# Chaining VectorE's weight halves, first subtractions and query gates, and projecting tokens one weight tile at a time, in a two-branch decoder layer

## The chip, the core and the metric

The kernel runs on one core of a Trainium2 chip. A core has a matrix engine (TensorE, "PE" in the profile, with its weight loads shown apart as "PEld"), a vector engine (VectorE, "DVE"), a scalar engine (ScalarE, "ACT"), GpSimd ("POOL") and the queue that issues most DMAs (SyncE, "SP"). Each engine runs its own instructions in order and waits for the others by semaphores. The metric is the device time of one execution in microseconds (us); the figure that counts is the median of several executions.

## What is computed

One decoder layer over 512 tokens of width 1024. After an RMS norm, one input projection feeds two branches and two merge gates; the branches are projected up, merged, projected out and added to the input, and a gated embedding is added last:

```
h  = rmsnorm(x)
(attention q, k, v, gate | recurrence f, q, value, gate | merge gates) = h @ W_in
A  = block_sparse_attention(qknorm(q), qknorm(k), v, bias) * silu(gate)   # 8 heads x 64
R  = rmsnorm(hgrn2(q, keys from f, value, decay from f)) * silu(gate)      # 4 heads x 128
x  = x + (sigmoid(ga) * (A @ Ua) + sigmoid(gb) * (R @ Ub)) @ W_o
x  = x + gate(x @ W_g) * (p @ W_p)
```

Everything is float32. In the recurrence, a head has a decay per token and channel; the kernel works with its cumulative logarithm, over four blocks of 128 tokens.

## The kernel before

**Products.** A float32 product is made as three reduced products. Every weight tile `wf` (512 KB, two buffers, loaded by SP) is split into an upper half `wh` (a copy on ScalarE, line 184) and a lower half `wl` (a subtraction on VectorE, line 185), three buffers each; inputs are split the same way (`xh`, `xl`). Then xh·wh, xl·wh and xh·wl are summed in a PSUM bank. `weight` hands out the tiles in one fixed sequence and prepares each two tiles ahead of its use, so that the halves of tile i wait until TensorE is done with tile i-3.

**Stages.** TensorE's order is the order in which the program is written. First come the token-by-feature projections `bi` (the recurrence's values) and `av` (the attention's values), then decay and query of recurrence head 0 (`bf0`, `bq0`), then `aq` and `ak` (the attention's queries and keys). `proj_tok` makes each of these four in four PSUM banks, one per block of 128 tokens, from four weight tiles; a tile gives 24 matmuls, two contraction chunks by three products by four token blocks. After that come the feature-by-token projections, one bank each (`mm3`, 24 matmuls per weight tile), in the order of a table: gates, then `bf` and `bq` of heads 1 to 3 in between. Last come the up projections, the output projection and the embedding.

**Work put between.** Recurrence and attention are generators. Every matmul of a projection advances a clock (`tick`, 0.227 us for a 128x512 matmul); a generator says with `yield` after how much of that clock it goes on, and its matmuls are then written at that place. For a recurrence head h, `hgrn_gates` (lines 410 to 433) makes the cumulative decay `hu` (scans, line 428), the keys `hk` and the gated query `hq` (line 431, which is also the last reader of the bank of `bq`). `hgrn_intra` makes, for blocks of 64, 32, 8 and 2 tokens, differences of `hu` (the first subtractions, lines 447, 448, 460, 481, 484), their exponentials on ScalarE, and products with key and query (lines 450, 453, 487, 490); then `hkd` (lines 510 to 512). Small matmuls fill two banks, `lpb` and `lpa`. From these a tile `s` is assembled with seven predicated copies on VectorE (line 496), and `sc` with copies on ScalarE (lines 543, 546) and GpSimd (line 556). `hgrn_out` transposes `hkd` (`hktp`, line 565; copied to `hkt`, line 568), makes the block states (`hds`, line 573; `st` on VectorE, lines 577 and 580), and then the output (`hop`, lines 586 and 588), which needs both `sc` and `st`. `hms` (lines 601, 602) sums squares for a norm.

An attention step makes scores `s` on TensorE (line 700), the exponentials and their scaling `p` (lines 707 to 711), transposes them (`pt`, line 718) and copies them (`ptS`, line 722).

**What orders the other engines.** TensorE's order is written by hand. In the `bi` stage ScalarE's, VectorE's and SP's are too. Elsewhere a scheduler orders ScalarE, VectorE, GpSimd and SP: it places, by a model of the times, the ready instruction with the highest priority, which is its place in the program; inside `high_priority(offset=AHEAD)` an instruction counts as written 150 places earlier. Weight halves, `hgrn_gates` and the attention's `p` stand in such blocks.

**PSUM.** Eight banks: four ("mm") go round the projections, so that projection i waits for the readers of projection i-4; two ("g") go round the recurrence, so that `hktp` takes the bank of `lpb`, `hds` that of `lpa`, and `hop` that of `hktp`; two ("a") the attention.

Of the kernel before, what the change touches and what calls it, by code (L numbers as in the profile page):

```python
# [11 lines left out]
F32 = mybir.dt.float32  # L12
R = mybir.dt.float32r
I32 = mybir.dt.int32
AF = mybir.ActivationFunctionType
OP = mybir.AluOpType
# [5 lines left out]
NT = S // 128  # L22
# [18 lines left out]
LD = 2  # L41
# [9 lines left out]
AHEAD = 150  # L51
# [6 lines left out]
def hybrid_layer_kernel(  # L58
# [121 lines left out]
        A.activation(lb[:, 5], lb[:, 4], AF.Ln)  # L180


    def split(hi, lo, src):
        A.activation(hi, src, AF.Copy)  # L184
        V.tensor_tensor(lo, src, hi.bitcast(F32), op=OP.subtract)  # L185
# [36 lines left out]
    def w_split(upto):  # L222
        while len(wtile) <= min(upto, len(wseq) - 1):
            i = len(wtile)
            w_load(i)
            ap, kn, cols = wseq[i]
            hi = unit("wh", f"wh{i}", R, (128, kn, cols))
            lo = unit("wl", f"wl{i}", R, (128, kn, cols))
            with tc.high_priority(offset=AHEAD):
                split(hi, lo, wraw[i])  # L230
            wtile.append((hi, lo))

    def weight(ap, ahead=LD):
# [134 lines left out]
    def proj_tok(g, name, xh, xl, between=None):  # L368
        banks = [bank("mm", f"{name}{t}") for t in range(NT)]
        for kp in range(4):  # L370
            if between:
                between(kp)
                w2 = [weight(w_tok[g, kp], 0)]
                order = [(0, kk, t) for kk in range(2) for t in range(NT)]
                if kp == 3:
                    order = [(0, kk, t) for t in range(NT) for kk in range(2)]
            elif kp % 2 == 0:
                w2 = [weight(w_tok[g, kp]), weight(w_tok[g, kp + 1])]
                order = [(k2, kk, t) for t in (0, 1) for k2 in range(2) for kk in range(2)]
                order += [(k2, kk, t) for t in (2, 3) for k2 in range(2) for kk in range(2)]  # L380
            else:
                continue
            for k2, kk, t in order:
                wh, wl = w2[k2]
                k = 2 * (kp + k2) + kk
                s_ = slice(t * 128, t * 128 + 128)
                for i, (a, b) in enumerate(((xh[k], wh), (xl[k], wh), (xh[k], wl))):
                    PE.matmul(banks[t], a[:, s_], b[:, kk, :], start=(k == 0 and i == 0),  # L388
                              stop=(k == KD - 1 and i == 2))
                tick(0.681)  # L390
        return banks
# [19 lines left out]
    def hgrn_gates(h, F, Q):  # L411
        a = unit("H", f"ha{h}")
        A.activation(a, F, AF.Abs)
        A.activation(a, a, AF.Exp, scale=-1.0)
        A.activation(a, a, AF.Ln, bias=onec[:, 0:1])
        um = unit("H", f"hu{h}")
        V.tensor_scalar(um, F, -1.0, 30.0, op0=OP.mult, op1=OP.min)
        A.activation(um, um, AF.Exp)
        A.activation(um, um, AF.Ln, bias=onec[:, 0:1], scale=lbv[:, h:h + 1])
        V.scalar_tensor_tensor(a, F, 0.0, a, op0=OP.min, op1=OP.subtract)  # L420
        kb = unit("H", f"hk{h}")
        V.tensor_tensor(kb, a, F, op=OP.subtract)
        A.activation(kb, kb, AF.Exp, bias=ln1mlb[:, h:h + 1])
        V.tensor_tensor(a, a, um, op=OP.add)
        cum = um
        for c in range(NT):
            s_ = slice(c * 128, c * 128 + 128)
            V.tensor_tensor_scan(cum[:, s_], onec.to_broadcast([128, 128]), a[:, s_], 0.0, OP.mult, OP.add)
        sigmoid(a, Q)
        qm = unit("QM", f"hq{h}", shape=(128, 16, 48))  # L430
        V.tensor_tensor(qm[:, :, 0:32], a.rearrange("p (g t) -> p g t", t=32), Q.rearrange("p (g t) -> p g t", t=32),
                        op=OP.mult)
        hg[h] = (kb, qm, cum)

    def hgrn_intra(h):
# [3 lines left out]
        def halves(b):  # L439

            x = unit("Q", f"hx{h}_{b}")
            n = S // (2 * b)

            def v(t, half):
                return t.rearrange("p (n two b) -> p n two b", two=2, b=b)[:, :, half, :]
            ref = v(cum, 0)[:, :, b - 1:b].to_broadcast([128, n, b])
            V.tensor_tensor(v(x, 0), ref, v(cum, 0), op=OP.subtract)
            V.tensor_tensor(v(x, 1), v(cum, 1), ref, op=OP.subtract)
            A.activation(x, x, AF.Exp)
            V.tensor_tensor(v(x, 0), v(kb, 0), v(x, 0), op=OP.mult)  # L450
            xq = x.rearrange("p (n two g t) -> p n two g t", two=2, t=32, g=b // 32)[:, :, 1]
            qq = q.rearrange("p (n two g) t -> p n two g t", two=2, g=b // 32)[:, :, 1]
            V.tensor_tensor(xq, qq, xq, op=OP.mult)
            return x

        def near():

            c2 = cum.rearrange("p (g n two) -> p g n two", n=16, two=2)
            o = qm[:, :, 32:48]
            V.tensor_tensor(o, c2[:, :, :, 1], c2[:, :, :, 0], op=OP.subtract)  # L460
            A.activation(o, o, AF.Exp)
            V.tensor_tensor(o, q.rearrange("p g (n two) -> p g n two", two=2)[:, :, :, 1], o, op=OP.mult)

        def fours(b):


            kx = unit("Q", f"hkx{h}_{b}")
            qx = unit("QX", f"hqx{h}_{b}", shape=(128, 16, 48))
            n, m = S // (4 * b), 8 // b
            parts = [(d, 4 - d, e * b) for d, e in ((1, 0), (2, 3), (3, 5))]  # L470
            k4 = kx.rearrange("p (n f t) -> p n f t", f=4, t=b)
            c4 = cum.rearrange("p (n f t) -> p n f t", f=4, t=b)
            b4 = kb.rearrange("p (n f t) -> p n f t", f=4, t=b)
            q4 = q.rearrange("p g (m f t) -> p g m (f t)", m=m, f=4)
            x4 = qx.rearrange("p g (m e) -> p (g m) e", m=m)
            y4 = qx.rearrange("p g (m e) -> p g m e", m=m)
            G.memset(k4[:, :, 3, :], 0.0)

            def end(w):
                return c4[:, :, 0:w, b - 1:b].to_broadcast([128, n, w, b])  # L480
            V.tensor_tensor(k4[:, :, 0:3], end(3), c4[:, :, 0:3], op=OP.subtract)
            for d, w, e in parts:
                o = x4[:, :, e:e + w * b].rearrange("p n (f t) -> p n f t", t=b)
                V.tensor_tensor(o, c4[:, :, d:4], end(w), op=OP.subtract)
            A.activation(k4[:, :, 0:3], k4[:, :, 0:3], AF.Exp)
            A.activation(qx, qx, AF.Exp)
            V.tensor_tensor(k4[:, :, 0:3], b4[:, :, 0:3], k4[:, :, 0:3], op=OP.mult)
            for d, w, e in parts:
                o = y4[:, :, :, e:e + w * b]
                V.tensor_tensor(o, q4[:, :, :, d * b:4 * b], o, op=OP.mult)  # L490
            return kx, qx
# [15 lines left out]
        kd = unit("KT", f"hkd{h}", shape=(128, 3 * 128))  # L507
        cv = cum.rearrange("p (c t) -> p c t", c=NT)
        k3 = kd.rearrange("p (c t) -> p c t", c=3)
        V.tensor_tensor(k3, cv[:, 0:3, 127:128].to_broadcast([128, 3, 128]), cv[:, 0:3, :], op=OP.subtract)  # L510
        A.activation(kd, kd, AF.Exp)
        V.tensor_tensor(kd, kd, kb[:, :3 * 128], op=OP.mult)
        yield 2.5
# [22 lines left out]
            PE.matmul(lnr[p_, c, :], kb[:, o:o + 32], qm[:, 4 * c + g, :], start=True, stop=True)  # L536
        cost(1.5)
        A.activation(cum, cum, AF.Exp)
        V.tensor_tensor(s32, lnr[:, :, 0:32], eye[:, None, :].to_broadcast([128, NT, 32]), op=OP.mult)
        scv = sc.rearrange("p (i two) t -> p i two t", two=2)  # L540
        for par in range(2):
            i = 64 * par
            A.activation(scv[0:64, :, par, 64:128], big[i:i + 64, 0:2, :], AF.Copy)
            for half in range(2):
                j = 64 * half
                A.activation(scv[j:j + 32, :, par, j + 32:j + 64], big[i + 32 * half:i + 32 * half + 32, 2:4, 0:32], AF.Copy)
        for i, b in ((4, 8), (1, 2)):
            for d, e in ((1, 0), (2, 3), (3, 5)):
                pred(i + d - 1, lambda t: t.rearrange("p c (m e) -> p c m e", m=8 // b)[:, :, :, d * b:4 * b],
                     l4[b].rearrange("p c (m e) -> p c m e", m=8 // b)[:, :, :, e * b:(e + 4 - d) * b])  # L550
        pred(0, lambda t: t.rearrange("p c (n two) -> p c n two", two=2)[:, :, :, 1], lnr[:, :, 32:48])
        q12 = q[:, 4:16]
        V.tensor_tensor(q12, q12, cum[:, 128:].rearrange("p (g t) -> p g t", t=32), op=OP.mult)
        for g in range(4):
            s_ = slice(32 * g, 32 * g + 32)
            G.tensor_copy(sc[s_, :, s_], s32[s_])
        hg[h] += (kd,)

    def hgrn_out(h, vb):
        kb, qm, cum, kd = hg[h][:4]  # L560
        nk = 3 * 128
        yield 3.5
        kt = bank("g", f"hktp{h}")
        for c in range(3):
            PE.transpose(kt[:, c * 128:c * 128 + 128], kd[:, c * 128:c * 128 + 128], ident)
# [449 lines left out]
```

## Time and profile before

| | |
|---|---|
| time, median of 3 executions (lowest, highest) | 473.75 us (473.58, 474.74) |
| the profiled execution's own time | 474.0 us |
| its span, first to last instruction | 471.9 us |
| TensorE's mean granted clock | 0.999 |
| busy: TensorE / VectorE / ScalarE / GpSimd | 464.6 / 310.8 / 273.9 / 14.2 us |

The profiled execution spends 2.1 us outside its span. In the views, `MATMUL aq<-wh,xh` is an instruction that reads `wh` and `xh` and writes `aq`; buffer and head numbers are left out, so `hq` is that of any head, and times tell which. In a timeline a row is the start, the duration, and the idle time ahead of it with what ended it. TensorE overlaps matmuls: a 128x512 row lasts 0.39 us, and the next one starts 0.23 us after it, so its lateness is read from starts.

### The profile page before, as it was taken

Reading aid. Unit: us, or ns where it says so; the run is one execution under the profiler, and the core shown is the slowest. Engines: PE = TensorE matmul, PEld = TensorE weight load, DVE = VectorE, ACT = ScalarE, POOL = GpSimd, SP = SyncE. Lnnn points to the kernel's source line nnn. Section 1 sums busy time; section 2 is a strip of 40 time slices with the busy share of each in tenths; the row PEclk is TensorE's granted clock in tenths of the full one; section 3 lists DMA queues with packets and bytes.
Section 4 is the critical chain, followed back from the end, with each engine's and each line's share of the span. In section 5 each row is a group of like instructions: output and inputs, shape, how many; then the busy total and the mean of one; then the engine's idle time right before and its main releaser. Section 6 shows DMA issues by size and latency. Waiting matters only on the chain.

```text
span 471.9 us, 7256 instructions
## 1 busy us (share of the span) xinstructions
PE 464.6 (98%) x2776; PEld 384.8 (82%) x2776; DVE 310.8 (66%) x615; ACT 273.9 (58%) x479; POOL 14.2 (3%) x34
## 2 busy tenths in 40 slices
PE   9999999999999999999999999999999999999996
PEld 7888877888888778888788888888878888888886
DVE  4769696668989799849995466434459854543332
ACT  5857683478598789748885676554344522243201
POOL 0005000000000010000000100000000000000000
PEclk9999999999999999999999999999999999999999
DMA  7642222221541423231422233112534544322211
GB/s 228 218 145 90 90 89 90 89 90 50 172 145 59 141 85 90 90 111 47 131 91 92 90 101 102 47 62 53 188 95 138 193 145 147 109 93 95 91 44 46
DMA packets 19027, 50.42 MB, mean 107 GB/s; under 512 B 2352, under 2 KB 2992, under 8 KB 18992
## 3 DMA queue, kind: packets, MB, share of 16 engines
q1 hardware_dynamic: 18848, 49.95, 33.1%
q8 instruction: 22, 0.36, 0.3%
q14 instruction: 13, 0.11, 0.1%
q10 hardware_dynamic: 144, 0.01, 0.0%
HBM read 45.75 MB, written 2.10 MB: 101 GB/s over the span
## 4 chain that ended last, share of the span: by engine, by line
PE 87%; DVE 6%; ACT 5%; issue 1%; POOL 0%; DVEq 0%; POOLq 0%
PE ga L246 9%; PE g L246 9%; PE h L246 9%; PE gb L246 7%; PE bi L388 5%; PE ua L246 5%; PE ak L388 5%; PE ub L246 5%; PE av L388 5%; PE bg L246 5%; PE bf L246 4%; PE ag L246 3%; PE aq L388 3%; PE pe L246 2%; PE o L733 2%; PE s L700 2%
## 5 line engine op out<-in xcount | busy, mean ns | idle before, releaser
L184 ACT ACTIVATE wh<-wf 128x1024 fp32r<-128x1024 f32 (+1 forms) x81 | 77.5, 957 | 106.0 <-PE h L246 19.1
L185 DVE TENSOR_TENSOR wl<-wf,wh 128x1024 fp32r<-128x1024 f32 (+1 forms) x81 | 89.8, 1111 | 48.4 <-ACT wh L184 47.9
L707 DVE CUSTOM_DVE_ANT_0 p<-s,bias 128x128 f32<-128x128 f32 (+3 forms) x32 | 15.0, 486 | 21.8 <-PE s L700 21.7
L709 ACT ACTIVATE p<-p,ps 128x128 f32<-128x128 f32 (+3 forms) x32 | 17.7, 554 | 19.5 <-DVE ps L707 19.5
L246 PE MATMUL g<-hh,wh 128*128 128x512 f32 (+1 forms) x72 | 26.3, 365 | 0.0
L246 PE MATMUL g<-hl,wh 128*128 128x512 f32 (+1 forms) x72 | 26.3, 365 | 0.0
L246 PE MATMUL g<-hh,wl 128*128 128x512 f32 (+1 forms) x72 | 26.3, 365 | 0.0
L246 PE MATMUL gb<-xh,wh 128*128 128x512 f32 x64 | 26.3, 411 | 0.0
L246 PE MATMUL ga<-xh,wh 128*128 128x512 f32 x64 | 25.6, 400 | 0.0
L246 PE MATMUL gb<-xh,wl 128*128 128x512 f32 x64 | 25.1, 393 | 0.0
L246 PE MATMUL ga<-xh,wl 128*128 128x512 f32 x64 | 25.0, 391 | 0.0
L246 PE MATMUL gb<-xl,wh 128*128 128x512 f32 x64 | 25.0, 391 | 0.0
L246 PE MATMUL ga<-xl,wh 128*128 128x512 f32 x64 | 25.0, 390 | 0.0
L246 PE MATMUL h<-mh,wh 128*128 128x512 f32 x64 | 24.9, 390 | 0.0
L246 PE MATMUL h<-ml,wh 128*128 128x512 f32 x64 | 24.9, 389 | 0.0
L246 PE MATMUL h<-mh,wl 128*128 128x512 f32 x64 | 24.9, 389 | 0.0
L722 ACT ACTIVATE ptS<-pt 128x384 f32<-128x384 f32 (+1 forms) x24 | 12.5, 521 | 10.0 <-PE pt L718 9.8
L903 DVE TENSOR_TENSOR hf<-h,xres 128x512 f32<-128x512 f32 x8 | 5.5, 691 | 18.1 <-PE h L246 18.1
L246 PEld LDWEIGHTS g<-hh,wh 128*128 128x128 f32 x72 | 13.6, 189 | 2.2
L246 PEld LDWEIGHTS g<-hh,wl 128*128 128x128 f32 x72 | 13.6, 189 | 2.2
L246 PEld LDWEIGHTS g<-hl,wh 128*128 128x128 f32 x72 | 13.6, 189 | 2.1
L945 DVE TENSOR_TENSOR sg<-sg,pe 128x512 f32<-128x512 f32 (+1 forms) x9 | 5.6, 625 | 14.4 <-ACT sg L944 12.1
(319 smaller groups left out, 1265.2 us busy)
## 6 DMA issues: line engine op xcount, KB each, us to landing
wf<-in_w_tr_dram SPq DMA_DIRECT2D x32, 512.0 KB, 3.4
wf<-in_w_tok_dram SPq DMA_DIRECT2D x15, 512.0 KB, 3.3
wf<-in_w_up_dram SPq DMA_DIRECT2D x16, 256.0 KB, 2.7
wf<-in_w_o_dram SPq DMA_DIRECT2D x8, 512.0 KB, 3.3
wf<-in_w_g_dram SPq DMA_DIRECT2D x8, 512.0 KB, 3.3
bias<-in_brow_dram SPq DMA_DIRECT2D x8, 256.0 KB, 3.4
xres<-in_xT_dram SPq DMA_DIRECT2D x8, 256.0 KB, 2.8
xr<-in_xT_dram SPq DMA_DIRECT2D x7, 256.0 KB, 5.5
```

The lines of the kernel that those rows point to most:

```text
L184: A.activation(hi, src, AF.Copy)
L185: V.tensor_tensor(lo, src, hi.bitcast(F32), op=OP.subtract)
L246: PE.matmul(ps, a[:, k, :], b[k], start=(n == 0), stop=(n == tot - 1))
L388: PE.matmul(banks[t], a[:, s_], b[:, kk, :], start=(k == 0 and i == 0), stop=(k == KD - 1 and i == 2))
L700: PE.matmul(sp[:, o:o + nk], qn[h][:, qs], k_[:, :nk], start=(i == 0), stop=(i == 1))
L707: V.tensor_tensor_reduce(p_, sp[:, o:o + nk], T[:, nk - 1::-1], -1.0, 3e38, OP.add, OP.min, st[:, 0:1])
L709: A.activation(p_, p_, AF.Exp, bias=st[:, 0:1], scale=-1.0, accum_out=st[:, 1:2])
L722: A.activation(pt, tp[:, :n * 128], AF.Copy)
L733: PE.matmul(o[64 * j:64 * j + 64, qs], va[kb][:, h0:h0 + 64], pts[2 * hp + j, i][:, o0 + kb * 128:o0 + kb * 128 + 128], start=(kb == 0), s ...
L903: V.tensor_tensor(t, ps, xres, op=OP.add)
L945: V.tensor_tensor(t[:, :w], t[:, :w], pe[:, s_], op=OP.mult)
```

## The change

Three things are changed; no operation is added or removed.

1. On VectorE, the lower halves of the weights, the gated query `hq`, the first subtractions and the subtraction of `hkd` are tied together in the order in which they are written: `pin` tells the scheduler that each comes after the one before. It adds no wait to the engine, it only fixes their mutual order.
2. `proj_tok` takes for `av`, `aq` and `ak` one weight tile at a time and goes over its four token blocks. Before, it took two tiles together: token blocks 0 and 1 with both, then 2 and 3 with both. `bi` stays as it is, and each projection still has 96 matmuls.
3. The assembling of `s` and `sc` at the end of `hgrn_intra` counts as written 150 places earlier, the GpSimd copies are written ahead of the product of line 553, and `hgrn_out` waits 5.0 instead of 3.5 us of the clock before `hktp`.

```diff
+    def pin(op):
+        if pinned[0] is not None:
+            tc.add_manual_dep(op.ins, pinned[0].name,
+                              mybir.DependencyInfo(mybir.DependencyClass.NoSync, mybir.DependencyReason.DATA))
+        pinned[0] = op.ins
...
             with tc.high_priority(offset=AHEAD):
-                split(hi, lo, wraw[i])
+                A.activation(hi, wraw[i], AF.Copy)
+                pin(V.tensor_tensor(lo, wraw[i], hi.bitcast(F32), op=OP.subtract))
...
-            elif kp % 2 == 0:
-                w2 = [weight(w_tok[g, kp]), weight(w_tok[g, kp + 1])]
-                order = [(k2, kk, t) for t in (0, 1) for k2 in range(2) for kk in range(2)]
-                order += [(k2, kk, t) for t in (2, 3) for k2 in range(2) for kk in range(2)]
...
+            wh, wl = weight(w_tok[g, kp], 0 if between else LD)
+            order = [(kk, t) for t in range(NT) for kk in range(2)]
...
-        V.tensor_tensor(qm[:, :, 0:32], a.rearrange("p (g t) -> p g t", t=32), Q.rearrange("p (g t) -> p g t", t=32),
-                        op=OP.mult)
+        pin(V.tensor_tensor(qm[:, :, 0:32], a.rearrange("p (g t) -> p g t", t=32),
+                            Q.rearrange("p (g t) -> p g t", t=32), op=OP.mult))
...
-            V.tensor_tensor(v(x, 0), ref, v(cum, 0), op=OP.subtract)
-            V.tensor_tensor(v(x, 1), v(cum, 1), ref, op=OP.subtract)
+            pin(V.tensor_tensor(v(x, 0), ref, v(cum, 0), op=OP.subtract))
+            pin(V.tensor_tensor(v(x, 1), v(cum, 1), ref, op=OP.subtract))
...
-        V.tensor_tensor(s32, lnr[:, :, 0:32], eye[:, None, :].to_broadcast([128, NT, 32]), op=OP.mult)
+        with tc.high_priority(offset=AHEAD):
+            V.tensor_tensor(s32, lnr[:, :, 0:32], eye[:, None, :].to_broadcast([128, NT, 32]), op=OP.mult)
...
-        yield 3.5
+        yield 5.0
         kt = bank("g", f"hktp{h}")
```

**VectorE while `aq` runs.** The two pieces are VectorE's instructions behind the scans of head 0. `wl12` and `wl13` are the lower halves of the third and fourth weight tile of `aq`; `hq0` at L431 (now L434) is the gated query. Before:

```order
L428 SCALAR_TENSOR_TENSOR hu0_600<-onec_85,ha0_596 128x128 x4
L510 TENSOR_TENSOR hkd0_870<-hu0_600 128x384
L185 TENSOR_TENSOR wl12_625<-wf12_622,wh12_624 128x1024
L447 TENSOR_TENSOR hx0_64_674<-hu0_600 128x4x64
...
L512 TENSOR_TENSOR hkd0_870<-hkd0_870,hk0_605 128x384
L431 TENSOR_TENSOR hq0_616<-ha0_596,bq0_571 128x16x32
...
L490 TENSOR_TENSOR hqx0_8_766<-hq0_616,hqx0_8_766 128x16x8
L462 TENSOR_TENSOR hq0_616<-hq0_616 128x16x16
L185 TENSOR_TENSOR wl13_631<-wf13_628,wh13_630 128x1024
L185 TENSOR_TENSOR wl14_692<-wf14_689,wh14_691 128x1024
```

Now:

```order
L431 SCALAR_TENSOR_TENSOR hu0_600<-onec_85,ha0_596 128x128 x4
L434 TENSOR_TENSOR hq0_616<-ha0_596,bq0_571 128x16x32
L240 TENSOR_TENSOR wl12_625<-wf12_622,wh12_624 128x1024
L240 TENSOR_TENSOR wl13_655<-wf13_652,wh13_654 128x1024
L450 TENSOR_TENSOR hx0_64_674<-hu0_600 128x4x64
L451 TENSOR_TENSOR hx0_64_674<-hu0_600 128x4x64
L453 TENSOR_TENSOR hx0_64_674<-hk0_605,hx0_64_674 128x4x64
L456 TENSOR_TENSOR hx0_64_674<-hq0_616,hx0_64_674 128x4x64
L240 TENSOR_TENSOR wl14_692<-wf14_689,wh14_691 128x1024
```

`hq0` stands right behind the scans instead of 17 rows later, `wl13` right behind `wl12` instead of 29 rows later, and the work of `hgrn_intra` comes after both.

**TensorE in head 1.** The transposition `hktp1` and what stands around it, at the change from `bq2` to `gb1`. Before:

```order
L700 MATMUL s12_1703<-kl1_1267,qs1_1004 128x384
L565 MATMUL hktp1_1714<-ident_87,hkd1_1575 128x128 x3
L246 MATMUL bq2_1588<-xh7_421,wh26_1467 128x512
L246 MATMUL bq2_1588<-xl7_422,wh26_1467 128x512
L246 MATMUL bq2_1588<-xh7_421,wl26_1468 128x512
L674 MATMUL ktp1_1723<-ident_87,kr0_1119 128x128
```

Now:

```order
L704 MATMUL s12_1703<-kl1_1267,qs1_998 128x384
L256 MATMUL bq2_1588<-xh7_415,wh26_1467 128x512
L256 MATMUL bq2_1588<-xl7_416,wh26_1467 128x512
L256 MATMUL bq2_1588<-xh7_415,wl26_1468 128x512
L256 MATMUL gb1_1745<-xh0_384,wh27_1524 128x512
L256 MATMUL gb1_1745<-xl0_385,wh27_1524 128x512
L256 MATMUL gb1_1745<-xh0_384,wl27_1525 128x512
L678 MATMUL ktp1_1749<-ident_87,kr0_1119 128x128
L678 MATMUL ktp1_1749<-ident_87,kr1_1124 128x128
L678 MATMUL ktp1_1749<-ident_87,kr2_1129 128x128
L678 MATMUL ktp1_1749<-ident_87,kr3_1134 128x128
L569 MATMUL hktp1_1766<-ident_87,hkd1_1575 128x128 x3
```

`hktp1` has moved behind six 128x512 matmuls and the four transpositions `ktp1`; `hds1` then follows twelve matmuls later, as before it followed after nine of `gb1` and the three of `bq2`.

**ScalarE in head 1.** The copies `hkt1` and `kh2`, the upper half `wh29` and the exponential of `p12`. Before:

```order
L722 ACTIVATE ptS03_1689<-pt03_1684 128x512
L568 ACTIVATE hkt1_1718<-hktp1_1714 128x384
L486 ACTIVATE hqx2_2_1975<-hqx2_2_1975 128x768
L184 ACTIVATE wh29_1764<-wf29_1762 128x1024
L251 ACTIVATE ha2_1740<-bq2_1588 128x512
L188 ACTIVATE kh2_1728<-ktp1_1723,sm_66 64x512
```

Now:

```order
L726 ACTIVATE ptS03_1689<-pt03_1684 128x512
L426 ACTIVATE hk2_1726<-hk2_1726,lb_95 128x512
L239 ACTIVATE wh29_1741<-wf29_1739 128x1024
L713 ACTIVATE p12_1706,ps12_1707<-p12_1706,ps12_1707 128x384
L261 ACTIVATE ha2_1717<-bq2_1588 128x512
L197 ACTIVATE kh2_1754<-ktp1_1749,sm_66 64x512
L572 ACTIVATE hkt1_1770<-hktp1_1766 128x384
```

`hkt1`, on which `hds1` waits, has moved from the front to behind `wh29`, the exponential, `ha2` and `kh2`.

More of the change, by code (lines that the diff above doesn't have):

```diff
@@ L180, in lower_bound @@
         A.activation(lb[:, 5], lb[:, 4], AF.Ln)
+    pinned = [None]
+    def pin(op):
[3 more added lines that the diff above has]
+        pinned[0] = op.ins
     def split(hi, lo, src):
@@ L372, in proj_tok @@
                 between(kp)
[L373 to L376, printed above, removed]
-            elif kp % 2 == 0:
-                w2 = [weight(w_tok[g, kp]), weight(w_tok[g, kp + 1])]
-                order = [(k2, kk, t) for t in (0, 1) for k2 in range(2) for kk in range(2)]
-                order += [(k2, kk, t) for t in (2, 3) for k2 in range(2) for kk in range(2)]
[L381 to L385, printed above, removed]
+            wh, wl = weight(w_tok[g, kp], 0 if between else LD)
+            order = [(kk, t) for t in range(NT) for kk in range(2)]
+            if between and kp < 3:
+                order = [(kk, t) for kk in range(2) for t in range(NT)]
+            for kk, t in order:
+                k = 2 * kp + kk
                 s_ = slice(t * 128, t * 128 + 128)
@@ L459, in near @@
             o = qm[:, :, 32:48]
-            V.tensor_tensor(o, c2[:, :, :, 1], c2[:, :, :, 0], op=OP.subtract)
+            pin(V.tensor_tensor(o, c2[:, :, :, 1], c2[:, :, :, 0], op=OP.subtract))
             A.activation(o, o, AF.Exp)
@@ L480, in end @@
                 return c4[:, :, 0:w, b - 1:b].to_broadcast([128, n, w, b])
-            V.tensor_tensor(k4[:, :, 0:3], end(3), c4[:, :, 0:3], op=OP.subtract)
+            pin(V.tensor_tensor(k4[:, :, 0:3], end(3), c4[:, :, 0:3], op=OP.subtract))
             for d, w, e in parts:
                 o = x4[:, :, e:e + w * b].rearrange("p n (f t) -> p n f t", t=b)
-                V.tensor_tensor(o, c4[:, :, d:4], end(w), op=OP.subtract)
+                pin(V.tensor_tensor(o, c4[:, :, d:4], end(w), op=OP.subtract))
             A.activation(k4[:, :, 0:3], k4[:, :, 0:3], AF.Exp)
@@ L509, in hgrn_intra @@
         k3 = kd.rearrange("p (c t) -> p c t", c=3)
-        V.tensor_tensor(k3, cv[:, 0:3, 127:128].to_broadcast([128, 3, 128]), cv[:, 0:3, :], op=OP.subtract)
+        pin(V.tensor_tensor(k3, cv[:, 0:3, 127:128].to_broadcast([128, 3, 128]), cv[:, 0:3, :], op=OP.subtract))
         A.activation(kd, kd, AF.Exp)
@@ L538, in hgrn_intra @@
         A.activation(cum, cum, AF.Exp)
-        V.tensor_tensor(s32, lnr[:, :, 0:32], eye[:, None, :].to_broadcast([128, NT, 32]), op=OP.mult)
[L540 to L551, printed above, removed]
+        with tc.high_priority(offset=AHEAD):
+            V.tensor_tensor(s32, lnr[:, :, 0:32], eye[:, None, :].to_broadcast([128, NT, 32]), op=OP.mult)
+            scv = sc.rearrange("p (i two) t -> p i two t", two=2)
+            for par in range(2):
+                i = 64 * par
+                A.activation(scv[0:64, :, par, 64:128], big[i:i + 64, 0:2, :], AF.Copy)
+                for half in range(2):
+                    j = 64 * half
+                    A.activation(scv[j:j + 32, :, par, j + 32:j + 64], big[i + 32 * half:i + 32 * half + 32, 2:4, 0:32], AF.Copy)
+            for i, b in ((4, 8), (1, 2)):
+                for d, e in ((1, 0), (2, 3), (3, 5)):
+                    pred(i + d - 1, lambda t: t.rearrange("p c (m e) -> p c m e", m=8 // b)[:, :, :, d * b:4 * b],
+                         l4[b].rearrange("p c (m e) -> p c m e", m=8 // b)[:, :, :, e * b:(e + 4 - d) * b])
+            pred(0, lambda t: t.rearrange("p c (n two) -> p c n two", two=2)[:, :, :, 1], lnr[:, :, 32:48])
+            for g in range(4):
+                s_ = slice(32 * g, 32 * g + 32)
+                G.tensor_copy(sc[s_, :, s_], s32[s_])
         q12 = q[:, 4:16]
         V.tensor_tensor(q12, q12, cum[:, 128:].rearrange("p (g t) -> p g t", t=32), op=OP.mult)
-        for g in range(4):
-            s_ = slice(32 * g, 32 * g + 32)
-            G.tensor_copy(sc[s_, :, s_], s32[s_])
         hg[h] += (kd,)
```

## The prediction

> **What bounds the kernel now.** I read the page first: busy times and the chain that ended last.
>
> ```profile
> PE 464.6 (98%) x2776; PEld 384.8 (82%) x2776; DVE 310.8 (66%) x615; ACT 273.9 (58%) x479; POOL 14.2 (3%) x34
> PEclk9999999999999999999999999999999999999999
> PE 87%; DVE 6%; ACT 5%; issue 1%; POOL 0%; DVEq 0%; POOLq 0%
> ```
>
> TensorE is busy 464.6 of 471.9 us at full granted clock in every slice. The change leaves its matmuls as they are, so it can only win back waits, of which there are at most 471.9 - 464.6 = 7.3 us, part of them at the start. The second view is TensorE's waits:
>
> ```profile
> PE aq L388 <- DVE wl L185: 0.9, 1, 0.9
> ...
> PE hop L586 <- POOL sc L556: 0.7, 1, 0.7
> PE hktp L565 <- DVE s L496: 0.5, 1, 0.5
> PE pt L718 <- DVE p L711: 0.4, 1, 0.4
> PE aq L388 <- DVE hq L431: 0.2, 1, 0.2
> ```
>
> Each is one event. The left-out one is the warm-up at the start, which the change doesn't touch. All five end on VectorE, the fourth GpSimd step standing itself behind VectorE's `s`. As matmuls overlap, idle time understates a delay; I take it from the starts in TensorE's timeline, an undisturbed 128x512 matmul starting 0.23 us after the one before (69.24 to 69.47):
>
> ```profile
> 61.53 0.39 PE L388 MATMUL aq<-wh,xh 128*128 128x512 f32 x1
> ...
> 69.24 0.39 PE L388 MATMUL aq<-wh,xl 128*128 128x512 f32 x1
> 69.47 0.39 PE L388 MATMUL aq<-wl,xh 128*128 128x512 f32 x1
> 70.01 0.50 PE L388 MATMUL aq<-wh,xh 128*128 128x512 f32 x1 [0.16 <-DVE hq L431]
> 70.35 0.39 PE L388 MATMUL aq<-wh,xl 128*128 128x512 f32 x1
> ...
> 74.46 0.39 PE L388 MATMUL aq<-wh,xl 128*128 128x512 f32 x1
> 75.78 0.50 PE L388 MATMUL aq<-wl,xh 128*128 128x512 f32 x1 [0.93 <-DVE wl L185]
> ...
> 84.98 0.39 PE L388 MATMUL ak<-wh,xh 128*128 128x512 f32 x1
> ```
>
> The first wait delays 70.01 - 69.47 - 0.23 = 0.31, and the matmul behind it comes 0.34 instead of 0.23 later, so 0.42. The second: 75.78 - 74.46 - 0.23 = 1.09, and with the same 0.11 behind it 1.20.
>
> **Part 1, `aq` (chain and single tiles).** Why these two were late, on VectorE and then on ScalarE:
>
> ```profile
> 69.28 0.68 DVE L431 TENSOR_TENSOR hq<-ha,bq 128x512 f32<-128x512 f32 x1
> ...
> 72.16 2.10 DVE L490 TENSOR_TENSOR hqx<-hq,hqx 128x384 f32<-128x384 f32 x6
> ...
> 74.51 2.35 DVE L185 TENSOR_TENSOR wl<-wf,wh 128x1024 fp32r<-128x1024 f32 x2
> ```
>
> ```profile
> 64.43 0.63 ACT L253 ACTIVATE ha<-ha 128x512 f32<-128x512 f32 x1
> ...
> 71.47 1.07 ACT L184 ACTIVATE wh<-wf 128x1024 fp32r<-128x1024 f32 x1 [1.21 <-PE aq L388]
> ```
>
> `aq3` takes the bank of `bq0`, whose last reader is `hq0`. `hq0` ran from 69.28 to 69.96, though its sigmoid was done at 64.43 + 0.63 = 65.06. Pinned right behind the scans it ends at 65.06 + 0.68 = 65.74 at the latest. But the single tile also brings `aq3` forward: not 36 but 18 matmuls into the stage, 61.53 + 18 x 0.227 = 65.6. So the wait is 0 to 0.2 plus 0.11 behind it; as `hkd0`'s exponential has left the middle of the sigmoid on ScalarE, I take 0. If something else delays the sigmoid by the length of a `wh`, it costs 1.1: the upper bound.
>
> `wl13` waits for `wh13`, which waits for TensorE to leave tile 10. In pairs it left that tile after 42 matmuls, at 71.4 (the row's releaser says so); alone it leaves it after 24, at 61.53 + 24 x 0.227 = 67.0. `wh13` then ends at 68.2 and `wl13`, no longer behind the products of `hqx0`, at about 69.5. Single tiles need it after 72 matmuls, at 77.9: 8 us to spare. Gain 1.20, and nothing in `ak` that should take its place: what moves behind `wl13`, `hgrn_intra` of head 0, has until `lpb0`, in the middle of `ak`, and I follow its products only to 88, some 4 us into it.
>
> `av` needs nothing either: `wl7` now falls between two steps of the norm and delays it by one half, 1.2, but the transposition of the norm stands 2.5 us behind its input and the last `xl` has 3 us.
>
> **Part 2, attention in head 1 (chain).** TensorE and, below it, VectorE:
>
> ```profile
> 155.08 0.39 PE L246 MATMUL bf<-xh,wl 128*128 128x512 f32 x1
> 155.83 0.52 PE L718 MATMUL pt<-ident,p 128*128 128x128 f32 x3 [0.37 <-DVE p L711]
> ```
>
> ```profile
> 155.27 0.42 DVE L711 TENSOR_SCALAR p<-p,ps 128x384 f32<-128x384 f32 x1
> ```
>
> Lateness 155.83 - 155.08 - 0.23 = 0.52. The scaling of `p02` stood behind `wl26`; a whole weight half costs
>
> ```profile
> L185 DVE TENSOR_TENSOR wl<-wf,wh 128x1024 fp32r<-128x1024 f32 x62 | 76.8, 1241 | 46.7 <-ACT wh L184 46.3
> ```
>
> 1.24 us, more than the lateness. In the new order it stands in front of `wl26` and of the products of the blocks of 8. Gain 0.52.
>
> **Part 3, `hktp1` (priority and yield).** TensorE, then VectorE:
>
> ```profile
> 167.86 0.34 PE L700 MATMUL s<-kl,qs 128*128 128x384 f32 x1
> 168.71 0.52 PE L565 MATMUL hktp<-ident,hkd 128*128 128x128 f32 x3 [0.51 <-DVE s L496]
> ```
>
> ```profile
> 166.38 0.69 DVE L424 TENSOR_TENSOR ha<-ha,hu 128x512 f32<-128x512 f32 x1 [0.30 <-ACT hu L419]
> ...
> 167.12 1.36 DVE L428 TENSOR_TENSOR_SCAN hu<-onec,ha 128x128 f32<-128x128 f32 x4
> 168.40 0.17 DVE L496 COPY_PREDICATED s<-mkf,lpb 128x32 f32<-128x32 int32 x1
> ```
>
> `hktp1` takes the bank of `lpb1` and waited for the third predicated copy, behind four scans; without the wait it would have started at 168.03, so 0.68 lost. It now comes six matmuls and four transpositions later: 168.03 + 6 x 0.23 + 0.44 = 169.8 (0.11 a transposition, from the three of `hktp1` that took 0.28 to the next start), against a copy that ends by 169.1 even behind all scans. Gain 0.68.
>
> What is late next is `hkt1`, on which `hds1` waits. `hds1` now comes at 169.8 + 0.28 + 12 x 0.23 = 172.8. ScalarE does ahead of it `wh29`, the exponential of `p12`, `ha2` and `kh2`:
>
> ```profile
> 169.27 0.49 ACT L568 ACTIVATE hkt<-hktp 128x384 f32<-128x384 f32 x1 [1.69 <-PE hktp L565]
> ...
> 170.57 1.04 ACT L184 ACTIVATE wh<-wf 128x1024 fp32r<-128x1024 f32 x1
> 171.53 0.57 ACT L251 ACTIVATE ha<-bq 128x512 f32<-128x512 f32 x1
> 172.00 0.67 ACT L188 ACTIVATE kh<-ktp,sm 64x512 fp32r<-64x512 f32 x1
> ...
> 173.61 0.61 ACT L709 ACTIVATE p<-p,ps 128x384 f32<-128x384 f32 x1
> ```
>
> With `hkt1` that is 1.04 + 0.61 + 0.2 (reading the sum) + 0.57 + 0.67 + 0.49 = 3.6 us. `wh29` can start when `bq2` is through (168.03 + 3 x 0.23 and about 0.2 to its end: 168.9), or up to 0.6 later if the exponential waits for VectorE: `hkt1` ends between 172.5 and 173.1. So `hds1` waits -0.3 to +0.3; if `wh29` starts no earlier than before (170.57), 174.2 and a wait of 1.3. Taken: 0.2.
>
> **Part 4, `hop2` (priority and yield).** TensorE, VectorE, GpSimd:
>
> ```profile
> 225.41 0.49 PE L718 MATMUL pt<-ident,p 128*128 128x128 f32 x3
> 226.57 0.71 PE L586 MATMUL hop<-sc,biv 128*128 128x128 f32 x4 [0.67 <-POOL sc L556]
> ```
>
> ```profile
> 224.83 0.29 DVE L496 COPY_PREDICATED s<-mkf,lpa 128x64 f32<-128x64 int32 x1
> ```
>
> ```profile
> 225.25 1.27 POOL L556 COPY sc<-s 32x128 f32<-32x128 f32 x4 [33.77 <-DVE s L496]
> ```
>
> Three transpositions take 0.24 to 0.28, so `hop2` was due at 225.65 and lost 0.92. In the new order the last predicated copy of `s2` no longer has a weight half ahead of it, and that alone (1.24) pays the 0.92; and `hop2` stands 13 matmuls, 2.9 us, later. The state `st2` is then the later of its two inputs: copied on VectorE about 4.2 us after `hds2` starts, and due 4.9 after it. Gain 0.92, with 0.7 to spare. For `hop1` the same sum leaves no more than 0 to 0.1, since `wl29` (1.24) stands ahead of `st1`. Heads 0 and 3 have over 2 us.
>
> **Sum.** 0.42 + 1.20 + 0.52 + 0.68 + 0.92 = 3.74 removed; 0.2 added at `hds1` and 0.0 to 0.1 at `hop1`: net 3.5. From the profiled execution's 474.0 that is 470.5; it lies 0.25 above the median, so on the median's footing 470.25. I write 470.3. The extreme where each part goes as well as it can, with a few of the 0.1 us gaps in `ak` going too, is 469.5.
>
> **Rivals.**
> *B, the recurrence's waits come back.* Only `aq` is cured (1.62), while `hds1`, `hop1` and `hop2` wait again, for `hkt` and `st` now, about as long as `pt02`, `hktp1` and `hop2` do today: 473.75 - 1.62 = 472.1. For it: the inputs now in question come from ScalarE and VectorE queues that hold a weight half right ahead of them, and slacks of 0 to 0.7 are less than one such half. Against: the scheduler's order leaves the five old delays with 1 us or more.
> *C, slower: a chained order that waits.* A pinned `wl` waits for its `wh`, and that for TensorE; all that stands behind it on VectorE waits along, the `p` and `st` that TensorE needs next too. A row above shows the mechanism: at 166.38 VectorE stood idle 0.30 for ScalarE, while predicated copies of finished banks stood behind. The price is a pair of halves, 1.04 + 1.24 = 2.3, for each place. Two such places in heads 1 to 3 eat the gain (4.6 - 3.7 = +0.9, 474.6), three make it slower: 6.9 - 3.7, 476.9. For it: VectorE has little room to catch up there,
>
> ```profile
> 136.59:196.00 59.41, 58.53 (x407) 48.49 (x406) 55.26 (x145) 49.52 (x98) 1.81 (x6) 1.00 0.30 95
> ```
>
> 55.26 busy of 59.41 us (third figure). Against: tile i needs only tile i-3 to be left, 5.4 us ahead of its own use, so that `wl` has 3 us even when it comes last. [...]
> *D, the change misses its places.* `aq3`, brought forward, waits on `hq0` for up to 1.1, and two of the other three gains are replaced: 1 us net, 472.7.
>
> **Numbers.** No change is what lies within 0.3% (1.42 us: 472.3 to 475.2), about what a measurement of this kernel can tell. The forecast has 0.60, B 0.20, D 0.11, C 0.09. Faster: the forecast, and of B and D together 0.13: 0.73. Slower: two thirds of C, and something unforeseen, 0.07. The same: 0.20. Eight in ten lie between 469.5 and 473.0, which takes in B and D and leaves out C; the forecast's own range is 469.5 to 471.5.
>
> **What would show it.** In TensorE's waits of the changed kernel the five rows above should be gone, and no row for `hds` or `hop` should exceed 0.3. `aq` should last 96 x 0.227 = 21.8 from its first start to that of `ak`, where it lasts 84.98 - 61.53 = 23.45 now; if it lasts 22.5, `hq0` is late (D). `wl13` should follow `wl12` at about 69.5. In head 1, `hkt1` should end within 0.3 of when `hds1` is due; if it ends at 174, ScalarE's order decides (B). A wait of `pt` or `s` on `p` or `ptS` of over 1 us in heads 1 to 3 with VectorE idle ahead of a `wl` would be C. What would make me wrong most easily is the hand-made time of `hkt1` and `st1`, whose slack is smaller than the error of such a reckoning.

## The result: 469.9 us, and the profile after

The changed kernel takes 469.90 us in the median of four executions (469.51 to 470.19), against 473.89 us before (473.58 to 474.74, four executions): a ratio of 0.9912, with a 95% interval of 0.9895 to 0.993. The forecast was 470.3. The profiled execution took 469.64 us, its span is 467.7 instead of 471.9. Of the page, the busy times and the chain that ended last:

```profile
PE 462.7 (99%) x2776; PEld 385.2 (82%) x2776; DVE 311.6 (67%) x615; ACT 274.6 (59%) x479; POOL 12.6 (3%) x34
...
PE 95%; DVE 2%; ACT 1%; DMA 1%; SPq 0%; issue 0%; DVEq 0%
```

All engines do the same instructions as before, in nearly the same busy time (GpSimd 12.6 for 14.2 us); VectorE and ScalarE have gone from 11% of the chain to 3%. TensorE's waits are now these two, the second of 0.2 us:

```profile
PE warm L147 <- PEq L1006: 0.8, 1, 0.8
PE hms L606 <- DVE htl L194: 0.2, 1, 0.2
```

All five rows on which the sum rested are gone, and a small one has come. TensorE's timeline of the changed kernel at the end of `bi`, at the start of `aq`, where `aq3` begins, at the start of `ak`, and at `hms0`:

```profile
27.54 0.39 PE L391 MATMUL av<-wh,gh 128*128 128x512 f32 x1
...
61.18 0.39 PE L391 MATMUL aq<-wh,xh 128*128 128x512 f32 x1
...
65.03 0.39 PE L391 MATMUL aq<-wl,xh 128*128 128x512 f32 x1
65.25 0.45 PE L391 MATMUL aq<-wh,xh 128*128 128x512 f32 x1
65.54 0.40 PE L391 MATMUL aq<-wh,xl 128*128 128x512 f32 x1
...
83.04 0.39 PE L391 MATMUL ak<-wh,xh 128*128 128x512 f32 x1
...
113.76 0.39 PE L605 MATMUL hms<-hth,ones 128*128 128x512 f32 x1
114.40 0.50 PE L606 MATMUL hms<-htl,ones 128*128 128x512 f32 x1 [0.25 <-DVE htl L194]
```

`aq` lasts 83.04 - 61.18 = 21.86 instead of 23.45: 1.59 of the 4.24 that TensorE's last matmul comes earlier. `hms0` gives back 0.27. The three waits of heads 1 and 2 (2.12 as forecast) and the small gaps around them make 2.47. And 0.36 lies in `bi`, which the change doesn't touch: there `av` starts at 27.54, and before at

```profile
27.90 0.39 PE L388 MATMUL av<-wh,gh 128*128 128x512 f32 x1
```

In the profiled execution of the kernel with the later `hms`, below, it starts at 27.98. This first stage, in which ScalarE waits for the first loads (at most 1.88 us before and 1.91 now, for `xr`), thus varies by some 0.4 us, and 0.36 of the profiled 4.24 is not the change's. Sum: 0.36 + 1.59 - 0.27 + 2.47 = 4.15, and the rest, 0.1, is spread over `ak` and the late stages.

### The profile page after: what moved, and what is told of

It reads as the page before. It is cut to its first block, busy times and chain, and to the rows that moved or that the text cites. A ratio compares the mean times of both kernels' runs of the same rounds, so it can differ in the third digit from the quotient of the medians.

```text
span 467.7 us, 7249 instructions
## 1 busy us (share of the span) xinstructions
PE 462.7 (99%) x2776; PEld 385.2 (82%) x2776; DVE 311.6 (67%) x615; ACT 274.6 (59%) x479; POOL 12.6 (3%) x34
## 4 chain that ended last, share of the span: by engine, by line
PE 95%; DVE 2%; ACT 1%; DMA 1%; SPq 0%; issue 0%; DVEq 0%
PE gb L256 9%; PE ga L256 9%; PE g L256 9%; PE h L256 9%; PE ua L256 5%; PE bq L256 5%; PE ub L256 5%; PE bf L256 5%; PE av L391 5%; PE aq L391 5%; PE ag L256 5%; PE bg L256 4%; PE bi L391 4%; PE ak L391 3%; PE pe L256 2%; PE s L704 2%
## 5 line engine op out<-in xcount | busy, mean ns | idle before, releaser
L239 ACT ACTIVATE wh<-wf 128x1024 fp32r<-128x1024 f32 (+1 forms) x78 | 75.8, 971 | 104.0 <-issue 20.1
L240 DVE TENSOR_TENSOR wl<-wf,wh 128x1024 fp32r<-128x1024 f32 (+1 forms) x78 | 87.7, 1126 | 49.9 <-ACT wh L239 47.3
```

What stands on the lines that cost most here:

```text
L239: A.activation(hi, wraw[i], AF.Copy)
L240: pin(V.tensor_tensor(lo, wraw[i], hi.bitcast(F32), op=OP.subtract))
```

## The experiments

Two theories stood against each other: that the three parts add up, each with its own share, and that each needs the others. A third was rival C of the prediction, a chained order that makes VectorE wait. The edits name the parts as the section on the change does.

### Single weight tiles alone

```diff
 # the kernel before, and in proj_tok:
+            wh, wl = weight(w_tok[g, kp], 0 if between else LD)
+            order = [(kk, t) for t in range(NT) for kk in range(2)]
```

> The kernel before with only the single weight tiles for av, aq and ak. Theory 1, the parts depend on each other: VectorE's order stays that of before, so the gated query hq0 still ends at about 69.9 us, behind the products, but aq3 now comes after 18 matmuls of aq instead of 36, at 65.6. It should wait some 4.3 us on hq0, while the wait on wl13 (1.2) goes: 473.9 + 4.3 - 1.2 - 0.4 (the old wait on hq0, contained in the new one) = 476.6, slower. Theory 2, the parts add up: the single tiles bring the 1.2 us of wl13 by themselves, 472.7.

Measured: 478.61 us, 1.01 of before (1.0085 to 1.0115). TensorE's timeline at `aq3`, and below it the granted clock (the last figure but two) in two windows:

```profile
64.80 0.39 PE L391 MATMUL aq<-wl,xh 128*128 128x512 f32 x1
69.44 0.79 PE L391 MATMUL aq<-wh,xh 128*128 128x512 f32 x1 [4.25 <-DVE hq L434]
70.03 0.63 PE L391 MATMUL aq<-wh,xl 128*128 128x512 f32 x1
70.45 0.63 PE L391 MATMUL aq<-wl,xh 128*128 128x512 f32 x1
```

```profile
60.00:64.80 4.80, 4.80 (x22) 3.95 (x22) 4.76 (x11) 4.29 (x7) 0.00 (x0) 1.00 0.20 61
...
69.50:74.80 5.30, 5.30 (x13) 4.17 (x14) 5.30 (x14) 1.24 (x2) 0.00 (x0) 0.51 0.00 0
```

Theory 1 holds: the wait is 69.44 - 64.80 - 0.23 = 4.41 long, and the one on `wl13` is gone. It cost 2.0 more than worked out, because behind the wait the clock was granted at 0.51 for about 5 us: a dozen matmuls started 0.43 instead of 0.23 us apart, 2.5 us more by their starts.

### The chain alone

```diff
 # the kernel before, and in w_split, hgrn_gates and hgrn_intra:
+            pin(...)   # weight halves, hq, first subtractions, hkd's subtraction
```

> The kernel before with only the chain on VectorE; token projections in pairs, priority and yield as before. Theory 1: hq0 comes right behind the scans (0.42 gained), p02 comes ahead of wl26 (0.52 gained). wl13 stands ahead of hgrn_intra but waits for wh13, which waits until TensorE leaves tile 10 after 42 matmuls (71.1 us); it then ends at about 73.5 and is due at 74.2, so the 1.2 go too, and VectorE stands idle for some 4 us ahead of it. hktp1 and hop2 wait as before (1.6). 473.9 - 2.1 = 471.8. Theory 2 (the single tiles carry the wl13 gain): 473.0. Theory 3 (a chained order that waits, rival C): the idle VectorE makes later work late, lpb0 above all, 474 or more.

Measured: 474.63 us, 1.0015 (1.0006 to 1.0024). VectorE in `aq`, then TensorE in `ak`:

```profile
65.53 1.22 DVE L240 TENSOR_TENSOR wl<-wf,wh 128x1024 fp32r<-128x1024 f32 x1
72.20 1.23 DVE L240 TENSOR_TENSOR wl<-wf,wh 128x1024 fp32r<-128x1024 f32 x1 [5.46 <-ACT wh L239]
```

```profile
97.62 0.55 PE L546 MATMUL lpa<-hq,hk 128*32 128x48 f32 x32 [2.00 <-DVE hq L472]
```

Theory 1 has `aq` right (both its waits and that of `pt02` are gone), but misses the price: VectorE stands idle 5.46 us ahead of `wl13`, `hgrn_intra` of head 0 comes that much later (its first subtractions, whose input `hu0` was done at 62.77, start at 73.34), and TensorE waits 2.0 us for its last product and about 0.6 for the queries (`qtp`). This is rival C, as theory 3 had it, though at `lpa0` and not at `lpb0`. `hktp1` waits 1.24 instead of 0.68, and `hop2`, which theory 1 left waiting, doesn't wait. Six of the ten executions, the median among them, had a mean clock of 0.996 and took 474.6 to 475.3 us; the four at 1.000 took 474.0 to 474.3, at most 0.4 over before.

### Priority and the later `hktp` alone

```diff
 # the kernel before, and at the end of hgrn_intra and in hgrn_out:
+        with tc.high_priority(offset=AHEAD):   # s and sc
-        yield 3.5
+        yield 5.0
```

> The kernel before with only the raised priority of the end of hgrn_intra, the GpSimd copies ahead of the product and the later hktp. Theory 1: hktp1 (0.68) and hop2 (0.92) stop waiting, pt02 and both waits of aq stay: 473.9 - 1.6 = 472.3; TensorE's waits list wl13, hq0 and p and neither s nor sc. Rival B (the recurrence waits on hkt or st instead): 473.5 or more, with a new row for hds or hop.

Measured: 474.36 us, 1.0004 (0.9995 to 1.0013), no difference. Of TensorE's waits, the recurrence's; then VectorE ahead of the state of head 2:

```profile
PE hop L599 <- DVE st L591: 1.3, 1, 1.3
...
PE hds L584 <- ACT p L720: 0.7, 1, 0.7
```

```profile
228.43 2.10 DVE L500 TENSOR_TENSOR hqx<-hq,hqx 128x384 f32<-128x384 f32 x6
...
230.90 0.35 DVE L591 SCALAR_TENSOR_TENSOR st<-st,hu,hds 128x128 f32<-128x128 f32 x1
```

Rival B holds for this part by itself. `hktp1` and the wait of `hop2` on `sc` are cured, and `hds1` waits 0.84 by its starts, `hop2` 1.5 on `st2`, whose last step stands behind six products of the next head. Without the chain the scheduler puts those products there; with it, `st2` is ready in time (224.57 below).

### Everything but the chain

```diff
 # the changed kernel, and all pin(...) taken off
```

> The changed kernel without the chain (single tiles, priority and yield kept). Theory 1: as with the tiles alone, aq3 waits some 4.3 us on hq0, and pt02 keeps its 0.5; hktp1 and hop2 stay cured: 476.6 - 1.6 = 475.0, 5 us over the changed kernel. Theory 2 (the parts add up): the chain's own share is hq0 and p02, 0.9, so 470.8.

Measured: 479.53 us, 1.0117 (1.0101 to 1.0134). The largest of TensorE's waits:

```profile
PE aq L391 <- DVE hq L434: 4.2, 1, 4.2
PE hop L592 <- DVE st L584: 1.3, 1, 1.3
...
PE hds L577 <- ACT p L713: 0.7, 1, 0.7
```

By its starts `aq3` waits 4.41 on `hq0`, with the clock at 0.52 for nine matmuls behind it, `pt02` 0.51, `hds1` 0.84, `hop2` 1.5. Theory 2 is out, and theory 1 is right about `aq3` and `pt02` but 4.5 us short: most of that is the low clock (about 1.7), `hop2`, which it took for cured, and `hds1`. The parts do not add up: the chain is worth 9.6 us here, and costs 0.7 by itself.

### Everything but the single tiles

```diff
 # the changed kernel, and proj_tok as before (pairs of tiles)
```

> The changed kernel with the token projections in pairs of tiles again (chain, priority and yield kept). Theory 1, from the run with the chain alone: wl13, chained ahead of hgrn_intra, waits for a tile that TensorE leaves late in pair order; VectorE idles some 4 us, and the small matmuls of lpa0 wait about 2.2 on hq0 and qtp about 0.5; all other waits stay away. 469.9 + 2.7 = 472.6. Theory 2, that the chain with priority is enough: 470 to 470.5.

Measured: 472.59 us, 0.9976 (0.9967 to 0.9985). The largest of its waits:

```profile
PE lpa L546 <- DVE hq L472: 2.0, 1, 2.0
```

with about 0.7 at `qtp`, and `pt02`, `hktp1`, `hds1` and `hop2` without a wait. Theory 1; that the median meets it to a hundredth is luck, as the ten executions run from 472.14 to 473.86. The single tiles pay for the chain: by themselves they remove no wait that the chain doesn't remove, but with them tile 10 is left earlier, and the chained `wl13` comes at 67.76 (shown below) instead of 72.35 here.

### Everything but priority and the later `hktp`

```diff
 # the changed kernel, and the end of hgrn_intra and the yield as before
```

> The changed kernel without its third part (priority, GpSimd copies and yield as before; chain and single tiles kept). Theory 1: hktp1 waits for the predicated copies as with the chain alone, 1.2 us, and hms0 no longer waits 0.4; hop2 doesn't wait: 469.9 + 1.2 - 0.3 = 470.8. Theory 2 (the third part is worth what it was forecast, 1.6): 471.5.

Measured: 470.93 us, 0.9944 (0.993 to 0.9959). VectorE, then TensorE in head 1:

```profile
164.98 1.36 DVE L431 TENSOR_TENSOR_SCAN hu<-onec,ha 128x128 f32<-128x128 f32 x4
166.26 0.17 DVE L499 COPY_PREDICATED s<-mkf,lpb 128x32 f32<-128x32 int32 x1
```

```profile
166.57 0.52 PE L568 MATMUL hktp<-ident,hkd 128*128 128x128 f32 x3 [1.07 <-DVE s L499]
```

Its only wait after the first stage. `hop2` doesn't wait although its place is the old one: the chain by itself has moved `s2` and `st2` forward. So the third part, forecast to bring 1.6 (`hktp1` and `hop2`), brings 1.0: the 1.24 at `hktp1`, less the 0.27 of `hms0`, which doesn't wait here.

### The changed kernel with the earlier `hktp`

```diff
 # the changed kernel
-        yield 5.0
+        yield 3.5
         kt = bank("g", f"hktp{h}")
```

> The changed kernel with only the yield ahead of hktp put back from 5.0 to 3.5 (raised priority kept). If the later place of hktp is what cures hktp1, it waits 0.5 to 1.2 for the predicated copies and the time is 470.4 to 471.1; if the raised priority alone is enough, the copies come earlier on VectorE and it stays at 469.9. hms0, which then comes earlier with its input, waits 0.2 instead of 0.4.

Measured: 470.35 us, 0.9926 (0.9911 to 0.9941); `hktp1` waits 0.61 and `hktp2` 0.32 on the predicated copies, `hms0` no longer. Of the 1.24 us at `hktp1`, the raised priority takes about half: the third predicated copy now stands behind two of the four scans. The later place takes the rest. The GpSimd copies, the remaining piece of the third part, were not tried alone.

### A later `hms`

```diff
 # the changed kernel
-        yield 3.5
+        yield 5.0
         ms = bank("g", f"hms{h}")
```

> The changed kernel with hms written 1.5 us of the clock later (yield 5.0 instead of 3.5 ahead of it), so that htl0 is done when hms0 is reached. The one wait left, 0.41 and 0.11 behind it, should go and nothing else come: 469.4. If the later hms makes the next step of the recurrence late (the two banks it goes round are held 2 us longer), a wait of lpb or lpa appears and the time is 469.9 or more.

Measured: 469.72 us (469.31 to 469.82), 0.991 of before (0.9893 to 0.9927). In the profiled execution no wait is left after `bi`, and between the start of `av` and the last matmul it is 0.47 us shorter than the changed kernel's. The medians, 469.72 and 469.90, lie too close together, beside a first stage that varies by 0.4, to call it faster.

### The chain without the weight halves, and that in pairs

```diff
 # the changed kernel, in w_split
-                pin(V.tensor_tensor(lo, wraw[i], hi.bitcast(F32), op=OP.subtract))
+                V.tensor_tensor(lo, wraw[i], hi.bitcast(F32), op=OP.subtract)
```

> The changed kernel, but the weight halves are left out of the chain (query gates and subtractions chained; single tiles, priority, yield kept). hq0 stands behind wl12, which can run while ScalarE makes the sigmoid, and p02 falls back behind wl26. If the chain's gain in aq comes from hq0 before the first subtractions' products, aq has no wait and pt02 waits 0.5 again: 470.5. If the weight halves in the chain carry it, hq0 or wl13 makes aq wait 1 us or more: 471 and up.

> As the last, and the token projections in pairs of tiles. If the 2.2 us that lpa0 waits with pairs and the whole chain come from VectorE standing idle ahead of the chained wl13, they go; wl13 falls back behind the products of hqx0 and makes aq wait about 1 us, pt02 0.5: 469.9 + 1.7 = 471.6. If they come from elsewhere in pair order, lpa0 still waits 2 us: 474.

Measured with single tiles: 470.90 us, 0.9939 (0.9924 to 0.9953); with pairs of tiles: 474.32 us, 1.0001 (0.9988 to 1.0013). TensorE's waits, of the first and of the second kernel:

```profile
PE pt L722 <- DVE p L715: 0.9, 1, 0.9
```

```profile
PE aq L398 <- DVE wl L240: 2.1, 1, 2.1
```

In both the weight halves are out of the chain, `hq0` is in time and `aq3` has no wait, so it is the order of `hq0` against the subtractions that cures it. The weight halves in the chain hold `p02` ahead of `wl26`; without them `pt02` waits 1.05 by its starts, where 0.5 was expected. With pairs the wait of `lpa0` is gone as expected and `wl13`, behind the products again, makes `aq` wait, 2.2 instead of the 1 us expected. One wait or the other: in these two runs with pairs, one of them is always there. Of the second kernel's ten executions four took 472.5 to 473.1 us, about the 469.9 + 2.2 + 1.05 of its waits; the other six took 474.2 to 474.6, at a mean clock of 0.996 instead of 1.000. One more execution of it took 473.08 us:

> The kernel of the last run but one once more, for one profiled execution: six of its ten executions took 474.2 to 474.6 us at a mean granted clock of 0.996, the other four 472.5 to 473.1 at 1.000. If the wait of 2.2 us on wl13 in aq is what lowers the clock, an execution of the longer kind shows a granted clock of about 0.5 for 3 to 4 us right behind that wait, and 128x512 matmuls 0.43 us apart there; if the clock falls elsewhere, the wait has nothing to do with it. An execution of the shorter kind leaves it open.

It was one of the shorter kind, so that stays open.

### The chain without the subtractions

```diff
 # the changed kernel, in hgrn_intra
-            pin(V.tensor_tensor(v(x, 0), ref, v(cum, 0), op=OP.subtract))   # and the other five
+            V.tensor_tensor(v(x, 0), ref, v(cum, 0), op=OP.subtract)
```

> The changed kernel with only weight halves and query gates chained, the subtractions and that of hkd left free. The scheduler then puts hgrn_intra's subtractions ahead of hq0 as before, and chains wl12 behind hq0. aq3 waits 4.3 us on hq0 and the granted clock falls for some 5 us behind it, as with the single tiles alone (2 us more); pt02 waits 0.5, hds1 0.8 and hop2 1.5 as without the chain: 479.5. If chaining hq0 with the weight halves is enough, 470 to 471.

Measured: 482.19 us, 1.0175 (1.0142 to 1.0208). TensorE's longest waits:

```profile
PE hop L592 <- DVE st L584: 3.6, 1, 3.6
PE aq L391 <- DVE hq L434: 3.4, 1, 3.4
```

Tying `hq0` to the weight halves doesn't bring it forward; it holds `wl12` back behind it. The 3.6 us at `hop2`, where 1.5 was expected, come from `st2`, whose last step now has a weight half ahead of it on VectorE, besides the products that are there without any chain. What brings `hq0` forward is that the subtractions may not pass it.

## Why the prediction was right, and where it was off

**The bound and the five waits: right.** TensorE's work didn't change, and all five waits went. The two of `aq` were forecast at 1.62 and brought 1.59; the working of `hq0` (at the latest 65.74, due 65.6) is met by VectorE's rows:

```profile
64.46 0.69 DVE L434 TENSOR_TENSOR hq<-ha,bq 128x512 f32<-128x512 f32 x1 [2.15 <-ACT ha L263]
65.07 1.22 DVE L240 TENSOR_TENSOR wl<-wf,wh 128x1024 fp32r<-128x1024 f32 x1
67.76 1.23 DVE L240 TENSOR_TENSOR wl<-wf,wh 128x1024 fp32r<-128x1024 f32 x1 [1.47 <-ACT wh L239]
```

It ended at 65.15 and `aq3` started at 65.25, 0.22 after the matmul ahead of it: the slack was a tenth of a microsecond at most, as thin as it was worked out. `wl13` ended at 68.99 for the 69.5 forecast; `aq` starts 0.35 earlier in this execution, so that this is 0.15 ahead of the forecast.

**`pt02`: right.** VectorE, then TensorE:

```profile
148.34 0.41 DVE L715 TENSOR_SCALAR p<-p,ps 128x384 f32<-128x384 f32 x1
148.67 1.21 DVE L240 TENSOR_TENSOR wl<-wf,wh 128x1024 fp32r<-128x1024 f32 x1
```

```profile
153.61 0.49 PE L722 MATMUL pt<-ident,p 128*128 128x128 f32 x3
```

The scaling of `p02` stands ahead of `wl26` and ended at 148.75, `pt02` started at 153.61.

**`hds1`, the 0.2 us added: didn't come.** ScalarE ahead of `hkt1`, then TensorE:

```profile
166.44 1.06 ACT L239 ACTIVATE wh<-wf 128x1024 fp32r<-128x1024 f32 x1 [0.56 <-PE bq L256]
...
169.52 0.47 ACT L572 ACTIVATE hkt<-hktp 128x384 f32<-128x384 f32 x1
```

```profile
166.02 0.39 PE L256 MATMUL bq<-xl,wh 128*128 128x512 f32 x1
166.25 0.40 PE L256 MATMUL bq<-xh,wl 128*128 128x512 f32 x1
...
167.60 0.49 PE L569 MATMUL hktp<-ident,hkd 128*128 128x128 f32 x3
...
170.67 0.83 PE L577 MATMUL hds<-biv,hkt 128*128 128x128 f32 x6
```

From the start of `wh29` to the end of `hkt1` are 169.99 - 166.44 = 3.55 us, forecast 3.6. But `wh29` didn't have to wait until `bq2` was through and 0.2 more: `bq2`'s last matmul started at 166.25, and it began 0.19 later, while 0.4 and up to 0.6 more had been allowed. The rows fit a simpler condition: `wh29` takes the buffer of `wh26`, whose last reader is not `bq2`'s last matmul (xh·wl) but the one before it (xl·wh), which ended at 166.02 + 0.39 = 166.41; `wh29` began at 166.44. So `hkt1` ended 0.68 before `hds1` started, outside the 0.3 either way that the forecast allowed. The mis-sized term is the start of `wh29`. `hop1`, for which 0.0 to 0.1 was added, doesn't wait either.

**`hop2`: right in size, wrong in its cause.** In head 2 (VectorE, GpSimd, TensorE):

```profile
224.57 0.73 DVE L584 SCALAR_TENSOR_TENSOR st<-st,hu,hds 128x128 f32<-128x128 f32 x2
```

```profile
218.35 1.27 POOL L558 COPY sc<-s 32x128 f32<-32x128 f32 x4 [28.35 <-DVE s L499]
```

```profile
225.98 0.60 PE L590 MATMUL hop<-sc,biv 128*128 128x128 f32 x4
226.43 0.28 PE L592 MATMUL hop<-hq,st 128*128 128x128 f32 x1
```

`sc` is done 6 us ahead and `st2` 0.7 ahead, the slack forecast. But the step was ascribed to priority and yield, and the kernel without them has no wait there either, nor has the chain alone, while priority and yield alone wait 1.5 on `st2`. The chain does it.

**What the sum missed.** It has no term for `hms0`: the over 2 us that the prediction grants head 0 are those of `hop`. `hms0` waits 0.41 by its starts instead of 0.16 for `htl0`, which stands behind a weight half on VectorE:

```profile
112.52 1.23 DVE L240 TENSOR_TENSOR wl<-wf,wh 128x1024 fp32r<-128x1024 f32 x1 [0.76 <-ACT wh L239]
113.66 0.69 DVE L194 TENSOR_TENSOR htl<-ht,hth 128x512 fp32r<-128x512 f32 x1
```

`hms0` is reached 1.27 us earlier than before, and `htl0` ends only 1.02 earlier (114.35). It cost 0.27. The 0.2 of `hds1` that didn't come and 0.35 of small gaps that went with the three waits, less the 0.27 of `hms0`, make 0.28 of the 0.4 us between forecast and median; the rest is less than the interval. That the total came so close is in part luck, as these small errors have opposite signs.

**The rivals.** B, given 0.20, is what happens without the chain; D's late `hq0`, given 0.11 and up to 1.1 us, comes with the single tiles alone, 4.41 us long. C, given 0.09, is what happens without the single tiles, at one place, in head 0, and for 2.7 us instead of the two or three places of 2.3 in heads 1 to 3 that it was priced at. In the working, a place of C cost a pair of halves; in the run it cost as much as the pair order keeps a tile. All three were forecast as accidents of the whole; the runs show them as what the parts do when one is missing. The prediction priced the whole and not the parts alone. Whoever reads its terms as what each part is worth by itself, 1.2 (tiles), 0.9 (chain) and 1.6 us (priority), is wrong by 5.9, 1.6 and 2.0 us.

## What to carry to other kernels

When two engines work from a fixed order, price a change of order by its slowest member: an instruction that is put early but waits for TensorE (here a weight half, ahead of which VectorE stood idle for 5.46 us with the chain alone) holds everything behind it, so move what releases its input together with it. A part that shows nothing or a loss when tried alone isn't thereby useless; here three parts measured +1.0%, +0.15% and 0.0% alone and -0.9% together. And after a row of waits has gone, look for the input that had been on time only because TensorE was late (`hms0`).

## What the runs showed of the hardware

In these runs TensorE's waits of 3.6 and 4.41 us in `aq` cost more than their length. Behind waits of 4.41 us (single tiles alone, and everything but the chain) the next 12 and 9 matmuls of 128x512 started some 0.43 instead of 0.23 us apart at a granted clock of 0.51 and 0.52, about 2.5 and 1.7 us on top. In the chain without the subtractions `aq3` is 3.6 us late by its starts (idle 3.44); there the matmuls behind it still started 0.23 apart for 1.0 us, and from 1.3 us on 0.43 apart seven times, at a clock of 0.50 (0.63 in the mean of the 4.6 us behind the wait). Behind waits of 1.5 us (`hop2`, priority alone) the clock stayed at 1.00.

What the clock does behind waits between 1.5 and 3.6 us is open. The kernel with pairs and the chain without weight halves has a wait of 2.2 us; of its ten executions four took 472.5 to 473.1 us at a mean clock of 1.000, six 474.2 to 474.6 at 0.996. The chain alone, with its wait of 2.0 us at `lpa0`, divides in the same way, four at 1.000 and six at 0.996, some 0.7 us apart. The profiled executions of both kernels have the clock at 1.00 behind the wait, so it isn't shown that the clock falls there in the others. If it does, the wait of 2.2 us costs an estimated 3.8 us in six of ten executions: its length, and the 1.6 us between the means of the two groups of times.
